# Rearranging the head of an RG-LRU and ConvFFN block: where modulation is applied, how the first product is cut, how the conditioning is spread

## The chip, the core and the metric

The kernel is one program on one core of a Trainium2 chip. The metric is the device time of one execution in microseconds (us), lower is better. Times are the median of several executions; the profile comes from one more execution of the same program.

## What is computed

One layer of a diffusion backbone: 256 context tokens and 1024 latent tokens of width 1024 go through an RMS norm, a shift and scale that depend on a conditioning vector, a bidirectional gated linear recurrence, and then a convolutional feed-forward part. Everything that the change touches stands in the first lines of it:

```python
silu_c, silu_cc = silu(c), silu(c_ctx)
sh1, sc1, g1, sh2, sc2, g2 = split(silu_c @ mod_w + mod_b, 6)      # 1024 values each
csh1, csc1, ...            = split(silu_cc @ mod_w + mod_b, 6)
h_lat = rms_norm(x)   * (1 + sc1)  + sh1
h_ctx = rms_norm(ctx) * (1 + csc1) + csh1
y_branch, x_branch = split(h @ w_in, 2)                            # 1280 columns each
xc = dwconv1d(x_branch)                                            # then gates, recurrence, gelu(y), w_out, FFN
```

## The kernel before

All products are made three times with operands split in a high and a low part (`hh`/`hl` for the activations, `wh`/`wl` for weights): high by high, low by high, high by low, summed in PSUM. Activations stand transposed: 128 of the 1024 channels on the partitions ("channel tile" k = 0 to 7), the 1280 tokens along the row (256 context, then 1024 latent).

The head (lines 183 to 315) runs under an order written out by hand for TensorE (PE), VectorE (DVE) and ScalarE (ACT); loads are issued in the program's order by SyncE (SP). It has these stages:

- **Conditioning rows** (L246 to L253, L277): DVE makes 16 diagonal tiles from `silu_c`, TensorE multiplies them with ones so that SiLU(c) and SiLU(c_ctx) stand on every partition, and four copies bring them from PSUM to the tiles `sh2` and `sc2`, which are free until later.
- **Norm and transposes** (L255 to L287): ten token tiles of 128 rows, in pairs. ACT squares and sums (L122), takes the root (L123), DVE refines it (L124, newton), DVE scales one tile of the pair (L267) and GpSimd (POOL) the other (L265), TensorE transposes (L270), and ACT and DVE copy the result from PSUM to `xT` (L231), a tile of 128 x 8 x 1280.
- **Modulation** of tile k (`mod_pe` L200, `mod_dve` L209): 16 pairs (k, shift or scale) are needed, each a product of a 1024 x 128 piece of `mod_w` with the two conditioning vectors. Seven pairs (`ON_PE`, L35) run on TensorE as eight matmuls 32 columns wide; nine run on DVE as two multiplications with a row sum (L213) and a small addition (L214).
- **Application and split** (`modulate`, L216): ACT applies shift and scale to context and latent part (L222, on `xT` in SBUF), rounds to `hh` (L223), and POOL, for tiles 6 and 7 DVE, makes `hl` (L85).
- **First product** `xp` (`k_step_late`, L162): per tile k nine matmuls over three chunks of tokens (512, 512, 256), first all with `hh,wh`, then `hh,wl`, then `hl,wh`. The first product of the other branch, `y0`, follows four tiles behind (`YLAG`, L313).

Then (L533) ACT takes `xp` into the convolution (L397), DVE adds the taps (L405), ACT and DVE split the result, the gates' products start (L423), `y0` goes through gelu (L388), the gates' sigmoids run (L434), and a long loop follows in which TensorE hardly pauses.

Of the kernel before, what the change touches and what calls it, by code (L numbers as in the profile page):

```python
# [11 lines left out]
F32 = mybir.dt.float32  # L12
# [7 lines left out]
P = 128  # L20
# [14 lines left out]
ON_PE = {(0, 0), (1, 0)} | {(k, 1) for k in (0, 1, 2, 4, 6)}  # L35
REP = 16

AHEAD_PE = 2
AHEAD_DVE = 2
YLAG = 4  # L40
LO_DVE = {6, 7}
# [25 lines left out]
def tile_kernel(ctx: ExitStack, tc: tile.TileContext, x, cx, par, mod_b, mod1, mod2, wyx, gw, w_out, w_up, w_down, fw, out):  # L67
# [39 lines left out]
    def newton(rs, sd, nv, between=lambda: None):  # L107

        V.reciprocal(rs, sd)
        between()  # L110
# [7 lines left out]
    def rstd_of(n, srcs, junks, between=lambda: None):  # L118
# [4 lines left out]
        ordered(act(sd, ss, AF.Sqrt, bias=eps, scale=1.0 / D))  # L123
        V.tensor_scalar(nv, ss, -0.5 / D, -0.5 * EPS, op0=ALU.mult, op1=ALU.add)  # L124
        newton(rs, sd, nv, between)
        return [rs[:, i:i + 1] for i in range(m)]

# [14 lines left out]
    ps_b = pool("ps_b", bufs=5, space=PSUM)  # L142
# [41 lines left out]
    xT = p0.tile([P, KD, NTOK], F32, name="xT")  # L184

    def head_load(src):
        t = p0.tile([P, D], F32, tag="ld", name="ld", bufs=8)
        load(t, src)
        return t

    def x_load(i):
        return head_load(cx[i * P:(i + 1) * P] if i < 2 else x[(i - 2) * P:(i - 1) * P])

    def mod_load(k):
        return [head_load(mod1[k, :, s * D:(s + 1) * D]) for s in range(2)]
# [4 lines left out]
    def mod_pe(k):  # L200
        for s in range(2):
            if (k, s) in ON_PE:
                i = 2 * k + s
                pm = pm_all[:, 2 * REP * i:2 * REP * (i + 1)]
                for kk in range(KD):
                    mm(pm.rearrange("p (r v) -> p r v", v=2), mr[k][s][:, kk * P:(kk + 1) * P], silu_c[:, kk].unsqueeze(1).to_broadcast([P, REP, 2]), kk == 0, kk == KD - 1)
                pms[k, s] = pm

    def mod_dve(k):  # L209
        for s in range(2):  # L210
            if (k, s) not in ON_PE:
                for v, row in enumerate((sh2, sc2)):
                    V.scalar_tensor_tensor(hl[KD - 1][:, :D], mr[k][s], 1.0, row, op0=ALU.mult, op1=ALU.mult, accum_out=md1[:, k, s, v:v + 1])  # L213
                V.tensor_scalar(md1[:, k, s], md1[:, k, s], mod_b1(k, s), None, op0=ALU.add)  # L214

    def modulate(k):  # L216
        for s in range(2):
            if (k, s) in ON_PE:
                act(md1[:, k, s], pms.pop((k, s))[:, :2], AF.Identity, bias=mod_b1(k, s))
        hf = xT[:, k]  # L220
        for v, t in ((1, slice(0, CTX)), (0, slice(CTX, NTOK))):
            act(hf[:, t], hf[:, t], AF.Identity, bias=md1[:, k, 0, v:v + 1], scale=md1[:, k, 1, v:v + 1])  # L222
        last[0] = S.copy(hh[k], hf).ins.name  # L223
        lo_part(V if k in LO_DVE else G, hl[k], hf, hh[k])

    def evac(p):

        for j, pts in zip((2 * p, 2 * p + 1), tps.pop(p)):
            for q, pt in enumerate(pts):
                o, pv = xT[:, 4 * q:4 * q + 4, j * P:(j + 1) * P], pt.rearrange("p (a b) -> p a b", a=4)  # L230
                (V.tensor_copy if j % 2 or q else S.copy)(o, pv)  # L231
                yield

    mr, pms, tps = {}, {}, {}

    def mod_start(k):
        mod_dve(k)
        mod_pe(k)

    with tc.manual_schedule(engines={ENG.PE, ENG.DVE, ENG.Activation}):  # L240
        act(silu_c, pr[:, C_C:].rearrange("p (t k) -> p k t", t=2), AF.Silu)

        act(stat[:, 0, :1], eps, AF.Sqrt)
        xts = [x_load(j) for j in range(4)]

        bp, _ = x_outs()  # L246
        bcs = [bp[:, :512], bp[:, 512:1024], bp[:, 1024:], bank()]
        for i, pb in enumerate(bcs):
            v, q = divmod(i, 2)
            for k in range(4):  # L250
# [665 lines left out]
```

## Time and profile before

| | us |
|---|---|
| median of 3 executions | 1283.44 (1283.37 to 1284.53) |
| the profiled execution | 1282.26 |
| its span in the profile | 1280.5 |
| TensorE busy | 1227.7 (96%) |
| VectorE busy | 1045.2 (82%) |
| ScalarE busy | 550.6 (43%) |
| GpSimd busy | 426.6 (33%) |
| mean granted TensorE clock | 0.982 of full |

The page's strip of 40 slices shows TensorE at 7, 8 or 9 tenths in the first three slices (32 us each) and nearly always 9 behind them. The head is the first 100 us; a row of the trace such as `79.43 1.42 ACT L397 ...` reads: start and length in us, engine, line, operation, output from inputs, shapes, and in brackets the idle time of the engine ahead of it and what ended that.

### The profile page before, as it was taken

How to read it: one execution, taken by the hardware profiler on the slowest of the kernel's cores; microseconds unless marked ns; L12 is line 12 of the kernel's file. 1: busy time of each engine (PE TensorE's matmuls, PEld its weight loads, DVE VectorE, ACT ScalarE, POOL GpSimd, SP SyncE). 2: the span in 40 equal slices, each digit the busy share in tenths (PEclk: the TensorE clock that was granted, in tenths of full speed). 3: DMA queues.
4: the chain of work that ended last, by engine and by line, in shares of the span. 5: the costliest groups of instructions: out<-in, count | busy, mean ns of one | idle time of the engine just before them, and what ended most of it. 6: DMA issues, size and time to landing. Idle time of an engine off the chain costs nothing.

```text
span 1280.5 us, 14366 instructions
## 1 busy us (share of the span) xinstructions
PE 1227.7 (96%) x5512; PEld 1000.2 (78%) x5512; DVE 1045.2 (82%) x1193; ACT 550.6 (43%) x707; POOL 426.6 (33%) x238
## 2 busy tenths in 40 slices
PE   7879999999998799999999999999999999999995
PEld 6758888888886578788888888888888888888873
DVE  7968999999988858679877777777777777777888
ACT  6568888888876234332222212222222222211344
POOL 4732222222223000252433333333333333334564
PEclk8799999999999899999999999999999999999999
DMA  8422333333334552221111111111111111111003
GB/s 319 176 82 83 123 124 124 123 124 123 108 99 149 193 171 79 66 83 50 35 48 50 50 50 50 50 50 50 50 50 47 39 38 43 50 50 50 17 1 131
DMA packets 56740, 108.74 MB, mean 85 GB/s; under 512 B 4568, under 2 KB 24024, under 8 KB 56672
## 3 DMA queue, kind: packets, MB, share of 16 engines
q1 hardware_dynamic: 56528, 107.57, 25.4%
q8 instruction: 43, 0.70, 0.2%
q10 hardware_dynamic: 144, 0.26, 0.1%
q14 instruction: 25, 0.20, 0.1%
HBM read 98.37 MB, written 9.44 MB: 84 GB/s over the span
## 4 chain that ended last, share of the span: by engine, by line
PE 83%; DVE 11%; ACT 3%; issue 2%; DMA 1%; POOL 0%; SPq 0%; DVEq 0%; ACTq 0%
PE u L88 38%; PE pd L88 20%; PE pb L88 14%; PE xp L88 10%; DVE hl L213 2%; DVE xc L405 1%; DVE md L214 1%; DVE stat L112 1%; DMA ld<-x_dram 1%; DVE rgl L85 1%; PE pt L720 0%; DVE x L790 0%; DVE b L461 0%; PE pb L270 0%; DVE o L860 0%
## 5 line engine op out<-in xcount | busy, mean ns | idle before, releaser
L757 DVE SCALAR_TENSOR_TENSOR acc<-u,pr,acc 128x945 f32<-128x945 f32 (+2 forms) x352 | 427.0, 1219 | 23.3 <-ACT acc L750 15.9
L88 PE MATMUL u<-h2h,wl 128*128 128x512 f32 x704 | 277.9, 395 | 0.0
L88 PE MATMUL u<-h2l,wh 128*128 128x512 f32 x704 | 277.4, 394 | 0.0
L88 PE MATMUL u<-h2h,wh 128*128 128x512 f32 x704 | 274.3, 390 | 0.2 <-ACT h2h L723 0.2
L85 POOL TENSOR_TENSOR wl<-raw,wh 128x1024 fp32r<-128x1024 f32 x66 | 161.6, 2449 | 329.1 <-ACT wh L150 311.1
L790 DVE TENSOR_TENSOR x<-pd,x 128x512 f32<-128x512 f32 x160 | 109.6, 685 | 128.6 <-PE pd L88 128.6
L88 PEld LDWEIGHTS u<-h2l,wh 128*128 128x128 f32 x704 | 132.4, 188 | 31.7 <-DVE h2l L85 0.4
L88 PEld LDWEIGHTS u<-h2h,wh 128*128 128x128 f32 x704 | 132.7, 189 | 31.1 <-ACT h2h L723 0.5
L88 PEld LDWEIGHTS u<-h2h,wl 128*128 128x128 f32 x704 | 132.4, 188 | 28.0
L88 PE MATMUL pd<-dh,gl 128*128 128x512 f32 x320 | 126.3, 395 | 0.0
L88 PE MATMUL pd<-dl,gh 128*128 128x512 f32 x320 | 126.2, 394 | 0.0
L88 PE MATMUL pd<-dh,gh 128*128 128x512 f32 x320 | 125.2, 392 | 0.0
L836 ACT CAST gh<-acc 128x1024 fp32r<-128x1024 f32 x22 | 23.1, 1050 | 223.7 <-DVE acc L833 223.7
L85 POOL TENSOR_TENSOR gl<-acc,gh 128x1024 fp32r<-128x1024 f32 x18 | 43.2, 2400 | 198.9 <-ACT gh L836 198.9
L832 ACT ACTIVATE acc<-acc 128x1024 f32<-128x1024 f32 x22 | 23.3, 1060 | 182.7 <-DVE acc L757 182.7
L150 ACT CAST wh<-raw 128x1024 fp32r<-128x1024 f32 x64 | 67.2, 1049 | 78.6 <-PE u L88 73.5
L88 PE MATMUL xp<-hh,wh 128*128 128x512 f32 (+1 forms) x240 | 84.9, 366 | 1.8 <-ACT hh L223 1.8
L88 PE MATMUL xp<-hl,wh 128*128 128x512 f32 (+1 forms) x240 | 82.0, 366 | 4.4 <-POOL hl L85 3.7
L88 PEld LDWEIGHTS pd<-dh,gl 128*128 128x128 f32 x320 | 60.0, 187 | 13.9
L88 PEld LDWEIGHTS pd<-dh,gh 128*128 128x128 f32 x320 | 60.1, 188 | 13.7
L88 PEld LDWEIGHTS pd<-dl,gh 128*128 128x128 f32 x320 | 60.0, 187 | 13.6
L769 POOL TENSOR_TENSOR dr<-dr,g 128x512 f32<-128x512 f32 x40 | 52.0, 1318 | 53.8 <-DMA dr<-w_down_dram 53.8
(188 smaller groups left out, 2284.6 us busy)
## 6 DMA issues: line engine op xcount, KB each, us to landing
raw<-w_up_dram SPq DMA_DIRECT2D x44, 512.0 KB, 3.4
mraw<-mod_dram SPq DMA_DIRECT2D x64, 256.0 KB, 4.4
raw<-wyx_dram SPq DMA_DIRECT2D x20, 512.0 KB, 3.6
dr<-w_down_dram SPq DMA_DIRECT2D x40, 256.0 KB, 4.4
ld<-mod_dram SPq DMA_DIRECT2D x16, 512.0 KB, 6.0
rgr<-rgd SPq DMA_DIRECT2D x16, 512.0 KB, 5.3
rgd<-r SPq DMA_DIRECT2D x10, 512.0 KB, 3.0
wor<-w_out_dram SPq DMA_DIRECT2D x10, 512.0 KB, 3.9
```

The source lines that it names most:

```text
L85: eng.tensor_tensor(lo, src, hi.bitcast(F32), op=ALU.subtract)
L88: T.matmul(o, w, r, start=start, stop=stop)
L112: V.scalar_tensor_tensor(sd, rs, rs, nv, op0=ALU.mult, op1=ALU.mult)
L150: S.copy(wh, raw)
L213: V.scalar_tensor_tensor(hl[KD - 1][:, :D], mr[k][s], 1.0, row, op0=ALU.mult, op1=ALU.mult, accum_out=md1[:, k, s, v:v + 1])
L214: V.tensor_scalar(md1[:, k, s], md1[:, k, s], mod_b1(k, s), None, op0=ALU.add)
L405: V.scalar_tensor_tensor(xc[:, oa:ob], xp[:, oa + s:ob + s], pr[:, C_CW + t * 4 + tap:C_CW + t * 4 + tap + 1], xc[:, oa:ob], op0=ALU.mult, ...
L757: V.scalar_tensor_tensor(o, uv[:, r0 + dy:r1 + dy, c0 + dx:c1 + dx], w(dy, dx), o, op0=ALU.mult, op1=ALU.add)
L769: G.tensor_tensor(raw, raw, g2[:, cs], op=ALU.mult)
L790: V.tensor_tensor(xs, pd, xs, op=ALU.add)
L832: ordered(act(aa, aa, AF.Silu))
L836: S.copy(gh, aa)
```

## The change

- The conditioning vectors come as a new input `cc`; two DMAs spread a row of 1024 values over the 128 partitions each, and ACT takes SiLU of the two tiles in place. The diagonal tiles, the ones products and the four copies are gone.
- `ON_PE` now holds (0, 0) and every (k, 1): nine pairs on TensorE, seven on DVE. Loads of `mod_w` pieces have five buffers of their own (`MODS`), token tiles ten. Pieces for tiles 0 and 1 are loaded ahead of, or between, the first four token tiles; the others two tiles ahead, with the later token tiles between them.
- Both halves of a token tile pair are scaled on DVE. The low parts of the activations and of the first two weights are made on DVE. POOL has no work in the head behind the identity.
- Nothing is copied from PSUM to `xT`: `turn(c, k)` transposes one channel tile of one chunk of tokens to PSUM, and `modulate(c, k, pt)` applies shift and scale from there to a small buffer `hf`, then rounds.
- The first product runs by chunks: chunk 0 for k = 0 to 7, chunk 1 from k = 3 on (`SECOND`), chunk 2 behind them. `y0` runs whole behind `xp`, one half of the latent tokens after the other.

```diff
-ON_PE = {(0, 0), (1, 0)} | {(k, 1) for k in (0, 1, 2, 4, 6)}
+ON_PE = {(0, 0)} | {(k, 1) for k in range(KD)}
+MODS = 5
+SECOND = {3: (0, 1), 4: (2, 3), 5: (4, 5), 6: (6,), 7: (7,)}
...
+    def turn(c, k):
+        a, n = CHUNKS[c]
+        pt = ps_h.tile([P, 512], F32, tag="pt", name="pt", bufs=4)
+        for i in range(n // P):
+            T.transpose(pt[:, i * P:(i + 1) * P], xts[a // P + i][:, k * P:(k + 1) * P], ident)
+        return pt
+
+    def modulate(c, k, pt):
+        a, n = CHUNKS[c]
+        hf = p0.tile([P, 512], F32, tag="hf", name="hf", bufs=3)
+        for v, lo, hi in ((1, a, min(a + n, CTX)), (0, max(a, CTX), a + n)):
+            if lo < hi:
+                act(hf[:, lo - a:hi - a], pt[:, lo - a:hi - a], AF.Identity, bias=md1[:, k, 0, v:v + 1], scale=md1[:, k, 1, v:v + 1])
+        last[0] = S.copy(hh[k][:, a:a + n], hf[:, :n]).ins.name
+        return hf
+
+    def low(c, k, hf):
+        a, n = CHUNKS[c]
+        lo_part(V, hl[k][:, a:a + n], hf[:, :n], hh[k][:, a:a + n])
...
+        for v, row in enumerate((sh2, sc2)):
+            load(row, cc[v:v + 1].to_broadcast([P, D]))
+            act(row, row, AF.Silu)
...
+        mod_load(0)
+        x_load(0)
+        x_load(1)
+        mod_load(1)
+        x_load(2)
+        x_load(3)
+        w_x = load_weight(NCH)
+        mod_pe(0)
+        mod_dve(0)
+        x_sums(0)
+        mod_pe(1)
+        x_scale(0)
+        mod_dve(1)
+        x_sums(1)
+        x_scale(1)
+        w_x = split(w_x, V)
...
+        for k in range(KD):
+            if k + 2 < KD:
+                mod_load(k + 2)
+            if k in (0, 1):
+                x_load(2 * k + 4)
+                x_load(2 * k + 5)
+            if k == 5:
+                x_load(8)
+                x_load(9)
+            if k == 6:
+                w_y = load_weight(0)
+            pt = turn(0, k)
+            hf = modulate(0, k, pt)
+            if 0 < k < KD - 1:
+                mod_pe(k + 1)
+                mod_dve(k + 1)
+            flush()
+            low(0, k, hf)
+            for kk in SECOND.get(k, ()):
+                pt = turn(1, kk)
+                hf = modulate(1, kk, pt)
+                low(1, kk, hf)
+                later.append(lambda kk=kk: x_step(1, kk))
+            x_step(0, k)
+            if k in (1, 2, 6):
+                p = {1: 2, 2: 3, 6: 4}[k]
+                x_sums(p)
+                x_scale(p)
+        pts = {k: turn(2, k) for k in range(2)}
+        flush()
+        for k in range(KD):
+            hf = modulate(2, k, pts.pop(k))
+            low(2, k, hf)
+            if k + 2 < KD:
+                pts[k + 2] = turn(2, k + 2)
+            x_step(2, k)
+        w_y = split(w_y, V)
...
+        for q in range(2):
+            for k in range(KD):
+                k_step(y0[q:q + 1], YS[q:q + 1], w_y, k)
```

`x_sums` is the squares and the root of a pair of token tiles, `x_scale` the refinement and the two scalings; `flush` issues the products of chunk 1 that were put off. Behind the head the instructions of all engines are the same and stand in the same order.

Two places show what moves. On TensorE, around channel tile 4 (`hh_94` is its high part, `hl_102` its low part, `hh_90` and `hl_98` are tile 0; `xp` is the first product, `pb` the other branch), before:

```order
L88 MATMUL xp<-hh_94,wh 128x512 x2
L88 MATMUL xp<-hh_94,wh 128x256
L88 MATMUL xp<-hh_94,wl 128x512 x2
L88 MATMUL xp<-hh_94,wl 128x256
L88 MATMUL xp<-hl_102,wh 128x512 x2
L88 MATMUL xp<-hl_102,wh 128x256
L88 MATMUL pb<-hh_90,wh 128x512
L88 MATMUL pb<-hl_98,wh 128x512
```

and now (`pt` takes transposes of token tiles; `pm` takes the modulation's products):

```order
L231 MATMUL pt<-ident,xt 128x128 x8
L86 MATMUL xp<-hh_94,wh 128x512
L86 MATMUL xp<-hh_94,wl 128x512
L86 MATMUL xp<-hl_102,wh 128x512
L231 MATMUL pt<-ident,xt 128x128 x4
L86 MATMUL pm<-silu_c,mr 128x32 x8
L86 MATMUL xp<-hh_92,wh 128x512
L86 MATMUL xp<-hh_92,wl 128x512
L86 MATMUL xp<-hl_100,wh 128x512
```

Nine products of one channel tile in a row have become three for chunk 0, with the transposes of the next tile right behind the product that needs the low part, and no product of the other branch between them. On ACT, around channel tiles 3 and 4, before (`md_71` holds shift and scale):

```order
L222 ACTIVATE xT<-xT,md_71 128x256
L222 ACTIVATE xT<-xT,md_71 128x1024
L223 CAST hh_93<-xT 128x1280
L219 ACTIVATE md_71<-pb,pr 128x2
L222 ACTIVATE xT<-xT,md_71 128x256
L222 ACTIVATE xT<-xT,md_71 128x1024
L223 CAST hh_94<-xT 128x1280
```

and now, from the two chunk-1 tiles (2 and 3) that go along with tile 4 to tile 5 of chunk 0:

```order
L240 CAST hh_94<-hf 128x512
L209 ACTIVATE md_71<-pm,pr 128x2
L239 ACTIVATE hf<-pt,md_71 128x512
L240 CAST hh_92<-hf 128x512
L239 ACTIVATE hf<-pt,md_71 128x512
L240 CAST hh_93<-hf 128x512
L239 ACTIVATE hf<-pt,md_71 128x256 x2
L240 CAST hh_95<-hf 128x512
```

Three instructions for a whole channel tile have become seven for its three chunks, spread over the head, and each now waits for a transpose.

## Rows read from the trace of the kernel before

**Rows 1.** Chain of waits in the first 100 us, shares by engine and line.
```profile
by line: DVE hl L213 31.8%; DVE md L214 9.6%; DMA ld<-x_dram 7.5%; PE pb L88 7.1%; PE xp L88 6.2%; PE pb L270 5.4%; DVE xc L405 4.8%; DVE xT L231 2.5%; POOL ld L265 2.4%; issue 2.2%; DVE ld L267 1.5%; ACT xh L411 1.4%; ACT xc L397 1.4%; DVE
```

**Rows 2.** A stretch: length; busy us of PE, PEld, DVE, ACT, POOL; clock, DMA share, GB/s.
```profile
40.00:60.00 20.00, 14.59 (x67) 12.48 (x66) 19.75 (x18) 8.72 (x10) 15.51 (x5) 0.76 0.38 127
```

**Rows 3.** Timeline, DVE's modulation and POOL's low parts, 50 to 61 us.
```profile
50.06 1.22 DVE L213 SCALAR_TENSOR_TENSOR hl<-ld,sh 128x1024 fp32r<-128x1024 f32 x1
52.72 1.22 DVE L213 SCALAR_TENSOR_TENSOR hl<-ld,sh 128x1024 fp32r<-128x1024 f32 x1
53.29 7.29 POOL L85 TENSOR_TENSOR hl<-xT,hh 128x1280 fp32r<-128x1280 f32 x2 [4.49 <-ACT hh L223]
53.99 3.80 DVE L213 SCALAR_TENSOR_TENSOR hl<-ld,sc 128x1024 fp32r<-128x1024 f32 x1
57.83 2.77 DVE L214 TENSOR_SCALAR md<-md,pr 128x2 f32<-128x2 f32 x1
```

**Rows 4.** Timeline, ACT and PE from the end of the first product.
```profile
79.43 1.42 ACT L397 ACTIVATE xc<-xp,pr 128x1280 f32<-128x1280 f32 x1 [2.52 <-PE xp L88]
85.71 0.63 PE L88 MATMUL pb<-hh,wl 128*128 128x512 f32 x2
88.56 1.09 ACT L388 ACTIVATE gy<-pb 128x512 f32<-128x512 f32 x2
93.54 1.63 ACT L434 ACTIVATE r<-pb,pr 128x512 f32<-128x512 f32 x3
94.28 0.38 PE L88 MATMUL pb<-xh,gwh 128*128 128x256 f32 x1 [2.16 <-ACT r L434]
```

**Rows 5.** Loads: one piece of the chain, and two stretches as in Rows 2.
```profile
2.58 7.54 DMA ld<-x_dram
10.00:12.00 2.00, 1.06 (x8) 0.85 (x8) 1.31 (x2) 1.93 (x7) 2.00 (x1) 1.00 1.03 420
531.00:532.00 1.00, 1.00 (x4) 0.81 (x3) 0.85 (x2) 1.00 (x3) 0.00 (x0) 0.50 0.99 283
```

**Rows 6.** Timeline, from the second square of the first pair to the first scaling.
```profile
7.60 1.06 ACT L122 ACTIVATE hh<-ld 128x1024 fp32r<-128x1024 f32 x1 [0.98 <-DMA ld<-cx_dram]
9.89 0.75 DVE L267 TENSOR_SCALAR ld<-ld,stat 128x1024 f32<-128x1024 f32 x1
```

**Rows 7.** Groups by shape: count, busy us and mean ns of one, idle ahead.
```profile
L750 ACT ACTIVATE acc<-u,pr 128x1024 f32<-128x1024 f32 x44 | 52.8, 1200 | 2.7 <-PE u L88 2.7
L397 ACT ACTIVATE xc<-xp,pr 128x1280 f32<-128x1280 f32 x10 | 14.2, 1417 | 2.5 <-PE xp L88 2.5
L411 ACT CAST xh<-xc 128x512 fp32r<-128x512 f32 x20 | 11.4, 619 | 6.0 <-DVE xc L405 6.0
L85 DVE TENSOR_TENSOR xl<-xc,xh 128x512 fp32r<-128x512 f32 x20 | 12.9, 688 | 2.1 <-ACT xh L411 1.5
```

**Rows 8.** Timeline, PE: transposes, narrow products, products in threes at either clock.
```profile
23.48 1.09 PE L270 MATMUL pb<-ident,ld 128*128 128x128 f32 x8 [0.59 <-POOL ld L265]
24.41 3.66 PE L88 MATMUL pb<-silu_c,ld 128*128 128x32 f32 x32
45.25 0.75 PE L88 MATMUL xp<-hl,wh 128*128 128x512 f32 x3
45.84 0.75 PE L88 MATMUL xp<-hh,wh 128*128 128x512 f32 x3
59.14 1.27 PE L88 MATMUL xp<-hl,wh 128*128 128x512 f32 x3
60.21 1.27 PE L88 MATMUL xp<-hh,wh 128*128 128x512 f32 x3
```

**Rows 9.** Stretches as in Rows 2, for the clock.
```profile
28.00:30.00 2.00, 1.99 (x13) 1.62 (x13) 0.67 (x1) 1.42 (x2) 0.00 (x0) 0.63 0.93 350
44.00:46.00 2.00, 2.00 (x12) 1.73 (x12) 2.00 (x3) 0.00 (x0) 2.00 (x2) 1.00 0.46 162
58.00:60.00 2.00, 2.00 (x8) 1.61 (x7) 2.00 (x1) 0.00 (x0) 2.00 (x1) 0.50 0.00 0
```

More of the change, by code (lines that the diff above doesn't have):

```diff
@@ L66, in tile_kernel @@
 @with_exitstack
[L67 removed]
+def tile_kernel(ctx: ExitStack, tc: tile.TileContext, x, cx, cc, par, mod_b, mod1, mod2, wyx, gw, w_out, w_up, w_down, fw, out):
     nc = tc.nc
@@ L123, in rstd_of, with rms_dve @@
         ordered(act(sd, ss, AF.Sqrt, bias=eps, scale=1.0 / D))
+    def rms_dve(n, m):
+        ss, nv, sd, rs = (stat[:, i, n:n + m] for i in range(4))
         V.tensor_scalar(nv, ss, -0.5 / D, -0.5 * EPS, op0=ALU.mult, op1=ALU.add)
-        newton(rs, sd, nv, between)
+        newton(rs, sd, nv)
         return [rs[:, i:i + 1] for i in range(m)]
+    def rstd_of(n, srcs, junks):
+        rms_act(n, srcs, junks)
+        return rms_dve(n, len(srcs))
     dr = ctx.enter_context(tc.tile_pool(name="dr", bufs=1, space=bass.MemoryType.DRAM))
@@ L183, in tile_kernel, with x_load @@
     p0 = pool("p0")
[L184 to L192, printed above, removed]
+    def x_load(j):
+        t = p0.tile([P, D], F32, tag="xt", name="xt", bufs=10)
+        load(t, cx[j * P:(j + 1) * P] if j < 2 else x[(j - 2) * P:(j - 1) * P])
+        xts[j] = t
     def mod_load(k):
-        return [head_load(mod1[k, :, s * D:(s + 1) * D]) for s in range(2)]
+        for s in range(2):
+            mr[k, s] = t = p0.tile([P, D], F32, tag="mr", name="mr", bufs=MODS)
+            load(t, mod1[k, :, s * D:(s + 1) * D])
     def mod_b1(k, s):
@@ L212, in mod_dve @@
                 for v, row in enumerate((sh2, sc2)):
-                    V.scalar_tensor_tensor(hl[KD - 1][:, :D], mr[k][s], 1.0, row, op0=ALU.mult, op1=ALU.mult, accum_out=md1[:, k, s, v:v + 1])
+                    V.scalar_tensor_tensor(hl[KD - 1][:, :D], mr[k, s], 1.0, row, op0=ALU.mult, op1=ALU.mult, accum_out=md1[:, k, s, v:v + 1])
                 V.tensor_scalar(md1[:, k, s], md1[:, k, s], mod_b1(k, s), None, op0=ALU.add)
[L216 to L238, printed above, removed]
+    def x_sums(p):
+        js = (2 * p, 2 * p + 1)
+        rms_act(2 * p, [xts[j] for j in js], [junk] * 2)
@@ L243, in tile_kernel @@
         act(stat[:, 0, :1], eps, AF.Sqrt)
[L244 to L250, printed above, removed]
-                dg = xT[:, i, k * P:(k + 1) * P]
-                V.tensor_scalar(dg, ident, silu_c[:, 4 * q + k, v:v + 1], None, op0=ALU.mult)
-                mm(pb[:, k * P:(k + 1) * P], ones, dg, True, True)
-        pm_all = bank()
@@ L303, in tile_kernel @@
[L303 to L314 removed]
+        pm_all = ps_h.tile([P, 512], F32, tag="pm", name="pm")
+        xp, xo0 = x_outs()
@@ new lines, in tile_kernel, with flush @@
+        junk = p0.tile([P, D], F32, tag="junk", name="junk")
+        mod_load(0)
[14 more added lines that the diff above has]
+        w_x = split(w_x, V)
+        later = []
+        def flush():
+            for f in later:
+                f()
+            later.clear()
```

81 lines of the change are left out of this document (14 added, 67 removed).

## The prediction

> **What bounds the kernel now.** I read the strip of 40 slices first: TensorE is short of work only in the first 100 us. So the question is when the dense part begins, and one event marks it: the first gate product that waits for a sigmoid, at 94.28 [rows 4]. From there on both kernels issue the same instructions in the same order and TensorE hardly pauses, so a shift of that event is the change of the time. Then the chain of waits [rows 1]: of the first 100 us 31.8% are DVE's L213 and 9.6% L214, the modulation's multiplications. A quiet pair (k, shift or scale) costs DVE 52.72 - 50.06 = 2.66 us; beside POOL's subtractions one multiplication takes 3.80 instead of 1.22 and the small addition 2.77, until POOL's instruction ends [rows 3]. Nine pairs should take 24 us, the chain gives them 41. DVE is therefore the bound in the middle of the head: 19.75 busy of 20 us, where ACT has 8.72 and TensorE runs at 0.76 of its clock [rows 2].
>
> **What goes, what comes, step by step.**
>
> *The start.* Before, the parameters and four tiles of 512 KB had landed at 2.58 + 7.54 = 10.1 us [rows 5]. Now the first five loads are the parameters, the two spread rows and the two pieces of tile 0: the same bytes to SBUF, so again 10.1 if a spread row goes like a tile. The only nearby stretch with a repeated source moved 283 GB/s where plain tiles reach 420 [rows 5]: 1.85 us a row instead of 1.25, 1.2 us for both; I take the lower price, since that stretch was shared with smaller loads, and keep +1.2 for the range. Six more loads at 1.25 us bring the pieces of tile 1 at 15.1 and the fourth token tile at 17.6. TensorE's eight narrow products of tile 1 (0.114 each [rows 8], at half clock 0.2) and the small ACT copy end at 17.1; ACT, in order, then takes two squares, and root, refinement and two scalings follow: a square of about 1.2, 2.3 from the start of the second to the scaling [rows 6], 1.5 for the scalings. First transposes at about 22.5, where before they came at 11. This wait for loads, with the modulations set between the token tiles, is the price of knowing the modulation early. The diagonal tiles, ones products and four copies that go, and the two SiLU that come (some 1.1 each on ACT), lie under these loads and count nothing; without that cover the SiLU would cost 2.2.
>
> *DVE.* Seven pairs are left, 7 x 2.66 = 18.6; low parts, 0.69 per 512 columns [rows 7], come to 11 for chunks 0 and 1 and 3 for chunk 2; five pairs of tiles are refined and scaled for some 2.3 each; two weights about 1.2 each. Together 47 where nothing of POOL holds it up, against 41 for the modulation alone before. The 17 us lost to POOL are gone, 12 of them are spent again on POOL's former work.
>
> *ACT.* Here the new bound forms. Activations out of PSUM with shift and scale: 1.200 for 1024 columns and 1.417 for 1280 [rows 7] give 0.77 for 512 and 0.55 for 256. With the cast (0.62 for 512, by the same slope 0.40 for 256) and an overlap of 0.1 between neighbours: chunk 0 (two of 256) 1.55, chunk 1 1.30, chunk 2 0.88 per channel tile; times eight 29.8. Six squares and three roots are still inside the loop, 8.4, and six small copies of the modulation, 1.0. Total 39.2 behind the first transposes.
>
> *The hand-offs.* ACT cannot work without a pause, since TensorE takes its instructions in order: transposes of tile k+1 stand behind the third product of tile k, which waits for DVE's low part. From ACT's cast to its next activation: 0.69 + a product + four transposes (1.09 for eight [rows 8]) + three hand-offs, 1.7 at full clock and 2.4 at half, where a group of three products takes 1.07 instead of 0.59 [rows 8]. Behind k = 0 this stands open, about 2.5. Behind k = 1 two squares cover it. At k = 2 DVE has the scaling of a pair and a modulation (5 us) ahead of the low part, the squares cover half: 2.6 open. For k = 3 to 6 the two chunk-1 tiles cover most of it, 1.2 open each, 5 in all. The entry to chunk 2 costs 1.1, its eight steps 0.1 each. Sum 12.
>
> So `xp` ends at 22.5 + 0.9 (first transposes) + 39.2 + 12 + 0.9 (last low part and product) = 75.5, against 79.4, where ACT takes it over [rows 4]: 3.9 us won.
>
> *The other branch gives most of it back.* Before, four of the eight tiles of `y0` lay in the pauses of the first product, and it ended at 85.71 + 0.63 = 86.3, 6.9 behind `xp`. Now all 48 products stand behind `xp`: 48 x 0.235 (0.59 buys 512, 512 and 256 columns) = 11.3; the weight's cast is the last of ACT's queue and its low part behind that on DVE, 1.3 until both are there. End 75.5 + 12.6 = 88.1, 1.8 later than before. Convolution, taps and split (8 us) lie under it. That DVE's subtraction for this weight stands ahead of the taps delays nothing TensorE waits for.
>
> *The end.* Before, from the end of the gelu (89.65) to the first sigmoid (93.54) 3.9 us of casts and table loads passed, and the gate product came 0.74 behind [rows 4]. Now the first half of `y0` is done 5.6 earlier, so table load and first gelu are over and only the second, 0.6, follows the end: 88.1 + 0.65 + 3.9 + 0.74 = 93.4. Against 94.28 that is 0.9 us won.
>
> *What costs nothing.* Pieces of `mod_w` wait for buffers that are freed one or two steps earlier, and the last two token tiles stand behind them in SP's queue, but are wanted two steps (10 us) later; cover gone, a load is 3 us. The loads of the long loop that stand ahead of the next weight in SP's queue delay it by some 3 us; TensorE wants it 14 us after `xp`.
>
> The profiled execution took 1282.26 (its span 1280.5), the median of three is 1283.44; a shift of 0.9 makes the two 1281.4 and 1282.5.
>
> **TensorE's clock is the large unknown.** In the trace it stands at half (0.50) at 58 to 60 us and at full at 44 to 46, and it fell at 28 to 30, behind 3.7 us of narrow products [rows 8, 9]. At full clock a step of k = 3 to 5 asks TensorE for 12 transposes, 8 narrow and 9 wide products: 1.4 + 0.9 + 2.1 = 4.4 us, beneath ACT's 5.4 with its pause; at half about 8, and TensorE is the bound: +2.5 a step. Before, unbroken groups of nine products stood at either clock (full at 45, half at 59 [rows 8, 9]); the first three steps now have three each, with pauses, so I take half clock until about 45 us and full behind it. If it is full from the start, the open hand-offs shrink and step 3 is shorter: 4.5 us better. If it comes back only at 60, three steps lose 2.5 less what pauses they had, about 5.5; at 70 or later chunk 2 and the first half of `y0` also suffer, 9.
> The Trainium skill (TensorE: Matmul & The Clock Gate, "HAM oscillation — how this bites in real kernels") says that bursts of products separated by waits fall back to the slow clock again and again, and advises long runs without waits; this change cuts runs up. Taken strictly, it gives the slow rival below; the trace so far bears it out in part, since products with pauses ran at full clock from 44 to 46.
>
> **Rivals.** (1) *Faster: the clock holds early.* It is back by 25 to 33 us, hand-offs run at the shorter price: 2.6 to 5.4 us won, 1278.0 to 1280.8. For it: from step 3 on transposes and products leave few pauses. Against it: the first three steps are thin, and squares and scalings lie between. Chance 0.33.
> (2) *Slower: the clock stays at half through steps 3 to 5.* TensorE becomes the bound of the loop; it decides from a return later than about 53 us: 2.6 to 8 us lost, 1286.0 to 1291.5. For it: narrow products stand in each step; a fall stands behind such ones [rows 9]. Against it: a TensorE that is the bound is also busy without pause, and before the full clock of 44 to 46 it had been so [rows 9]. Chance 0.19.
> (3) *The modulation is not known ahead.* Loads decide: if spread rows take 1.85 or more and pieces come later than the tiles, the first transposes move to 24 or 25 and DVE's chain is still what ACT waits for: 2 us more than forecast, 1284.5, a little slower than before but within the bound. Chance 0.06.
> (4) *Forecast:* -0.9, with hand-offs and durations 2 us off either way, 1280.9 to 1286.0. Chance 0.42.
>
> **How the numbers follow.** About 0.2%, 2.6 us, is what a measurement of this kernel can tell from no change. Faster: rival 1 and a bit of the forecast's edge, 0.34. Slower: rival 2 and the edge of 3, 0.21. Same: 0.45. The range runs from rival 1's end, 1278.0, into rival 2 up to 1287.5, which leaves out about a tenth there and less below. I predict 1282.5.
>
> **What would show it.** First transposes near 22.5 (later than 24: rival 3). ACT's idle time between 23 and 76 near 12, most of it ended by transposes. `xp` over at 75.5, `y0` 12.6 behind it. No multiplication of DVE over 1.3 in the head. The granted clock near 0.5 up to 45 and 1.0 behind. The forecast is wrong if the first waiting gate product starts outside 91.7 to 96.9, or if anything behind it differs between the two traces by more than 1 us.

## The result: slower by 0.56%, and the profile after

The changed kernel took 1290.99 us (median of 4, 1288.64 to 1291.55) against 1283.4 (4, 1282.21 to 1284.53): ratio 1.0056, 95% interval 1.0038 to 1.0073. The forecast was 1282.5 with a range of 1278.0 to 1287.5. The profiled execution took 1291.4, its span is 1289.6 (before 1282.26 and 1280.5), 9.1 us more. One execution of a later run, with one scale pair more on TensorE, took 1370.11 at a granted clock of 0.84 and is left out of that run's numbers.

The event that the forecast watched, the first gate product that waits for a sigmoid, came at 103.12 in place of 94.28 [rows 4]: 8.84 later, so nearly the whole difference lies ahead of it. The event is not the time itself, though: behind it the profiled executions of the kernels below take 1183.9 to 1187.7 us (before 1186.2, after 1186.5), so a shift of the event can differ from the shift of the time by up to some 2 us, and both are given. The timeline of ACT and TensorE from the end of the first product, after (start, duration, instruction, idle time and what ended it):

```profile
85.52 1.42 ACT L411 ACTIVATE xc<-xp,pr 128x1280 f32<-128x1280 f32 x1
...
97.88 0.60 ACT L402 ACTIVATE gy<-pb 128x512 f32<-128x512 f32 x1 [2.62 <-PE pb L86]
...
103.12 0.39 PE L86 MATMUL pb<-xh,gwh 128*128 128x256 f32 x1 [0.36 <-ACT r L448]
```

The first product is handed over at 85.52, ten us later than the 75.5 of the forecast; from there on the distances are those of the forecast. So the miss lies in the start and in the loop over the channel tiles. The chain of waits of the first 100 us, after, says where to look; it stands against [rows 1]:

```profile
by line: PE pm L86 21.2%; PE pb L86 11.0%; DMA mr<-mod_dram 8.7%; PE xp L86 8.0%; ACT hf L239 8.0%; PE pt L231 6.6%; issue 5.1%; DVE hl L215 4.8%; DMA xt<-x_dram 4.8%; ACT junk L119 4.6%; DVE xt L224 3.6%; DVE hl L83 2.5%; ACT wh L154 2.0%;
```

DVE's multiplications fell from 31.8% to 4.8% (L215), as intended. In their place stands `pm`, 21.2%: the narrow products on TensorE that compute the modulation, which the forecast had as a small cost. The stretches of the loop (length; busy us and count of PE, PEld, DVE, ACT, POOL; clock, DMA share, GB/s) answer to [rows 2]:

```profile
20.00:40.00 20.00, 13.63 (x54) 11.51 (x53) 12.73 (x32) 11.69 (x24) 0.00 (x0) 1.00 0.66 257
40.00:60.00 20.00, 18.16 (x94) 16.36 (x94) 15.30 (x31) 12.30 (x24) 0.00 (x0) 1.00 0.49 154
60.00:80.00 20.00, 16.48 (x91) 12.58 (x91) 13.45 (x27) 16.00 (x32) 0.00 (x0) 0.91 0.20 78
```

From 40 to 60 us DVE went from 19.75 to 15.30 and TensorE from 14.59 to 18.16: most of the work moved from DVE to TensorE. ACT, which the forecast took for the new bound, has 12.30 of 20 there.

Now TensorE's timeline, after: the three narrow groups of the start, the first transposes, three of the loop's narrow groups, and two neighbouring wide products at either clock:

```profile
10.91 3.59 PE L86 MATMUL pm<-silu_c,mr 128*128 128x32 f32 x16 [10.91 <-DMA mr<-mod_dram]
14.86 3.62 PE L86 MATMUL pm<-silu_c,mr 128*128 128x32 f32 x16 [0.35 <-ACT md L209]
18.83 3.62 PE L86 MATMUL pm<-silu_c,mr 128*128 128x32 f32 x16 [0.35 <-ACT md L209]
...
23.04 1.05 PE L231 MATMUL pt<-ident,xt 128*128 128x128 f32 x2 [0.59 <-DVE xt L224]
...
28.46 0.47 PE L231 MATMUL pt<-ident,xt 128*128 128x128 f32 x1 [0.19 <-DVE xt L224]
...
32.99 3.46 PE L86 MATMUL pm<-silu_c,mr 128*128 128x32 f32 x16
...
51.73 0.63 PE L86 MATMUL xp<-hh,wl 128*128 128x512 f32 x1
52.16 0.63 PE L86 MATMUL xp<-hl,wh 128*128 128x512 f32 x1
...
56.14 0.40 PE L86 MATMUL xp<-hl,wh 128*128 128x512 f32 x1
56.38 0.39 PE L86 MATMUL xp<-hh,wh 128*128 128x512 f32 x1
...
59.09 1.87 PE L86 MATMUL pm<-silu_c,mr 128*128 128x32 f32 x16
...
65.29 1.87 PE L86 MATMUL pm<-silu_c,mr 128*128 128x32 f32 x16
```

Read the counts at the line ends. One pair (one tile, shift or scale) is eight calls in the source, and x16 in the trace. So the "eight matmuls" of a pair in the description of the kernel before are sixteen for TensorE. A pair costs 1.87 at full clock and 3.46 to 3.62 at half, where the forecast had 0.9 and 1.6 (eight at 0.114 and at 0.2). The row to see it in was there before: the group by shape of the narrow products, of before and of after, has 112 for seven pairs and 144 for nine.

```profile
L88 PE MATMUL pb<-silu_c,ld 128*128 128x32 f32 x112 | 16.9, 315 | 4.2 <-ACT md L219 4.2
```

```profile
L86 PE MATMUL pm<-silu_c,mr 128*128 128x32 f32 x144 | 27.3, 359 | 11.6 <-DMA mr<-mod_dram 10.9 <-ACT md L209 0.7
```

### The profile page after: what moved, and what is told of

The parts are those of the page before. It is cut to its first block, busy times and chain, and to the rows that moved or that the text cites. A ratio compares the mean times of both kernels' runs of the same rounds, so it can differ in the third digit from the quotient of the medians.

```text
span 1289.6 us, 14368 instructions
## 1 busy us (share of the span) xinstructions
PE 1234.5 (96%) x5512; PEld 1003.9 (78%) x5512; DVE 1027.1 (80%) x1179; ACT 557.1 (43%) x736; POOL 387.1 (30%) x225
## 4 chain that ended last, share of the span: by engine, by line
PE 86%; DVE 7%; ACT 3%; DMA 2%; issue 2%; SPq 0%; POOL 0%; DVEq 0%; ACTq 0%
PE u L86 38%; PE pd L86 20%; PE pb L86 15%; PE xp L86 10%; PE pm L86 2%; DMA mr<-mod_dram 1%; DVE stat L109 1%; ACT hf L239 1%; PE pt L734 1%; DVE x L804 1%; DVE rgl L83 1%; PE pt L231 1%; DVE b L475 0%; DVE o L874 0%; DVE xc L419 0%
## 5 line engine op out<-in xcount | busy, mean ns | idle before, releaser
L83 POOL TENSOR_TENSOR wl<-raw,wh 128x1024 fp32r<-128x1024 f32 x64 | 156.8, 2449 | 323.9 <-ACT wh L154 300.1
L86 PE MATMUL xp<-hh,wh 128*128 128x512 f32 (+1 forms) x240 | 89.1, 371 | 4.3 <-ACT hh L240 4.2
L86 PE MATMUL xp<-hl,wh 128*128 128x512 f32 (+1 forms) x240 | 85.2, 368 | 2.9 <-DVE hl L83 2.9
L783 POOL TENSOR_TENSOR dr<-dr,g 128x512 f32<-128x512 f32 x40 | 52.2, 1324 | 58.5 <-DMA dr<-w_down_dram 50.1
```

The source lines that it names most:

```text
L83: eng.tensor_tensor(lo, src, hi.bitcast(F32), op=ALU.subtract)
L86: T.matmul(o, w, r, start=start, stop=stop)
L783: G.tensor_tensor(raw, raw, g2[:, cs], op=ALU.mult)
```

## The experiments

Theory N: the narrow groups are the miss. They cost twice the forecast; three of them stand in a row in the start, one more stands ahead of the wide products in each of the steps k = 1 to 6, and the longer half-clock stretch is their consequence. The rivals: C, the first product cut in threes, with a hand-off behind each three, is what costs; L, the loads of the spread rows; K, half of the loss is the slow clock of the thin first steps. Each experiment is an edit of the changed kernel unless it says otherwise.

**Half of the narrow products.** Every second product of a pair is left out, and with it half of the modulation's sum; the run is for its time alone.

```diff
-                for kk in range(KD):
+                for kk in range(0, KD, 2):
...
-... kk == 0, kk == KD - 1)
+... kk == 0, kk == KD - 2)
```

> The changed kernel with every second of the eight partial products of a modulation pair on TensorE left out (the modulation is therefore not the reference's), so that a pair is 8 recorded narrow products instead of 16, which is what the forecast counted. Theory N (the forecast's miss is this count: the trace of before has 112 narrow products for seven pairs, 16 each): a pair takes about 1.75 us at half clock instead of 3.6, the first transposes of the last token tile move from 28.5 to about 23 to 24.5, xp ends near 76.5 instead of 85.5, the first gate product that waits for a sigmoid starts near 94.5 instead of 103.1, and the time is 1281 to 1285. Rival C (the first product cut in threes with a hand-off behind each is what costs): that product starts at 100 or later, the time is 1287 or more. Rival L (the loads of the spread rows): the start moves by less than 2 us.

Measured: 1282.73 (8 runs), ratio 0.9997 (0.9986 to 1.0007). Its narrow products by shape, and from the timelines the first pair, the transposes of the fourth token tile, the first narrow group at full clock, the hand-over of the first product, the second gelu and the event:

```profile
L86 PE MATMUL pm<-silu_c,mr 128*128 128x32 f32 x72 | 13.9, 350 | 12.2 <-DMA mr<-mod_dram 11.9 <-ACT md L209 0.4
```

```profile
9.65 1.88 PE L86 MATMUL pm<-silu_c,mr 128*128 128x32 f32 x8 [9.65 <-DMA mr<-mod_dram]
...
23.78 0.47 PE L231 MATMUL pt<-ident,xt 128*128 128x128 f32 x1 [0.18 <-DVE xt L224]
...
45.27 0.98 PE L86 MATMUL pm<-silu_c,mr 128*128 128x32 f32 x8
...
75.44 1.42 ACT L411 ACTIVATE xc<-xp,pr 128x1280 f32<-128x1280 f32 x1
...
87.81 0.60 ACT L402 ACTIVATE gy<-pb 128x512 f32<-128x512 f32 x1 [2.63 <-PE pb L86]
...
93.05 0.39 PE L86 MATMUL pb<-xh,gwh 128*128 128x256 f32 x1 [0.36 <-ACT r L448]
```

With the count that the forecast used, the forecast's steps come out: 75.44 for 75.5, 87.8 for 88.1, 93.05 for 93.4, 1282.7 for 1282.5. That they agree so closely is in part luck: the fourth token tile's transposes come at 23.78 for 22.5, and the loop behind them is as much shorter than forecast. ACT's wait for transposes, which was to be near 12 between 23 and 76, is 12.5 from 22 to 76. The clock is back at about 45, as forecast, and not at 55: its late return in the changed kernel followed from the groups. C is out, which wanted the event at 100 or later, and L, which wanted the start moved by less than 2 us: the fourth tile's transposes moved by 4.7. Theory N holds for nearly all of the miss: against the kernel before, measured beside each, the medians are 7.6 us above (changed kernel), 0.1 above (this run) and 0.9 below (forecast), so 7.5 of 8.5 us. The event moves by 10.1, of which 1.3 are loads that came earlier in this profiled execution (9.65 for 10.91).

**Two columns in place of 32.** The run above takes away products and work alike. This one keeps the count:

```diff
-REP = 16
+REP = 1
```

> The changed kernel with 2 columns in place of 32 in each narrow product; nothing is left out, the number of products stays (16 recorded to a pair). Theory W (a narrow product is paid by its columns): a pair falls to under half, 0.9 at full and under 1.8 at half clock, and the loss goes as in the run with half the products: event 92 to 95, time 1281 to 1284. Theory F (a price for each instruction, whatever its columns): a pair stays at 1.5 to 1.9 at full and 3 to 3.6 at half, event 101 to 104, time 1289 to 1291.5. Rival C (with so few columns the clock stays at half longer): a pair shorter, but products 0.43 apart beyond 55 us, event over 98.

Measured: 1290.17 (4 runs), ratio 1.0059 (1.0042 to 1.0076), event 102.29. The group by shape, one pair at full clock with its weight loads (PEld is TensorE's weight load), and the weight loads of such a pair in the changed kernel with its 32 columns:

```profile
L86 PE MATMUL pm<-silu_c,mr 128*128 128x2 f32 x144 | 26.7, 316 | 10.4 <-DMA mr<-mod_dram 9.7 <-ACT md L209 0.7
```

```profile
57.48 1.84 PE L86 MATMUL pm<-silu_c,mr 128*128 128x2 f32 x16
57.37 1.86 PEld L86 LDWEIGHTS pm<-silu_c,mr 128*128 128x128 f32 x16
```

```profile
58.98 1.87 PEld L86 LDWEIGHTS pm<-silu_c,mr 128*128 128x128 f32 x16
```

A sixteenth of the columns, and a pair costs 1.84 in place of 1.87: theory F. What a narrow product costs is not its columns. Its stationary operand is a piece of `mod_w` of 128 x 128 that no other product uses, and sixteen loads of weights fill the same 1.86 us without a gap. That fits a price per load of weights of 0.116 at full clock (1.86 / 16) and some 0.22 at half (3.46 and 3.62 / 16). It is an inference: a fixed price for each such product, whatever its weights, fits as well, since no run here took the loads away and kept the products. The Trainium skill (TensorE: Matmul & The Clock Gate, "LDWEIGHTS (loading the stationary operand)") says that a load is paid by the columns of the weights; by its formula 128 of them are an estimate of 128 / 1.2 = 107 ns. If the price is the load's, the 0.116 at full clock agrees roughly, the 0.22 at half does not.

**The start in another order.** Token tiles are loaded ahead of the pieces, and the sums of both pairs of tiles stand ahead of the narrow groups:

```diff
-        mod_load(0)
         x_load(0)
         x_load(1)
-        mod_load(1)
+        mod_load(0)
         x_load(2)
         x_load(3)
+        mod_load(1)
         w_x = load_weight(NCH)
-        mod_pe(0)
-        mod_dve(0)
         x_sums(0)
-        mod_pe(1)
         x_scale(0)
-        mod_dve(1)
         x_sums(1)
         x_scale(1)
+        mod_pe(0)
+        mod_dve(0)
+        mod_pe(1)
+        mod_dve(1)
```

> The changed kernel with the order of its start alone changed: token tiles 0 and 1, then the pieces of channel tile 0, tiles 2 and 3, pieces of tile 1; squares and scalings ahead of the modulation on ACT and DVE. Theory N: the squares no longer stand on ACT behind the copies of three narrow pairs, first transposes at 23 to 24 instead of 28.5, the loop behind is unchanged, the first waiting gate product 4 to 5 us earlier (98 to 99.5), time 1286 to 1287.5. Rival C (hand-offs of the loop set the end): the loop gives the start back, the product moves by less than 1.5 us, time 1289.5 to 1291.

Measured: 1288.71 (5 runs), ratio 1.0041 (1.0026 to 1.0055).

```profile
24.46 1.09 PE L231 MATMUL pt<-ident,xt 128*128 128x128 f32 x4
...
61.20 1.93 PE L86 MATMUL pm<-silu_c,mr 128*128 128x32 f32 x16
...
63.95 0.63 PE L86 MATMUL xp<-hl,wh 128*128 128x512 f32 x1
64.38 0.63 PE L86 MATMUL xp<-hh,wh 128*128 128x512 f32 x1
...
100.85 0.38 PE L86 MATMUL pb<-xh,gwh 128*128 128x256 f32 x1 [0.40 <-ACT r L448]
```

The transposes of the fourth token tile come 4.0 earlier (24.46 for 28.46), the event 2.3: between what the two theories expected. The 4.0 last to the end of the loop: its last narrow group starts at 61.20 for 65.29. Behind it products stand 0.43 apart (63.95, 64.38), at half clock, where the changed kernel had its full clock, and 1.7 us are lost (from the fourth tile's transposes to the event 100.85 - 24.46 = 76.4 against 103.12 - 28.46 = 74.7). So what the start won lasted, and the clock took part of it back in this execution, the slowest of the five; the others were not profiled. How much the order wins is less sure: in three later runs that keep the changed kernel's start the same transposes came at 26.54, 26.96 and 27.11, so it is 2.1 to 4.0. What it is due to stays open between the loads, ACT's squares behind copies that wait for narrow groups, and DVE's scalings behind a modulation, since the edit moves all three.

**The clock alone.** Fourteen wide products on constants ahead of the loop, into `xp` before it is used:

```diff
         w_x = split(w_x, V)
+        for _ in range(14):
+            mm(xp[:, :512].rearrange("p (r v) -> p r v", v=P), ones_r, ones_r.unsqueeze(1).to_broadcast([P, 4, P]), True, True)
```

> The changed kernel with 14 wide products (ones by ones, into a bank that the first product overwrites) on TensorE between the narrow pairs of tiles 0 and 1 and the first transposes, where TensorE waits for the scalings: at half clock 14 x 0.43 = 6 us, from 22.5 to 28.5, so nothing waits for them. If the slow clock of the first five steps is half of the loss (theory K): products in the loop start at full clock (0.235 apart instead of 0.43) at once, a narrow pair takes 1.87 instead of 3.46 in steps 1 to 4, and the first waiting gate product comes 4 to 8 us earlier, at 95 to 99, time 1283 to 1287. If the narrow pairs pull the clock down again at once (N with its own clock effect), the full clock lasts one or two steps at most and the product comes 0 to 3 us earlier.

Measured: 1288.27 (3 runs), ratio 1.0045 (1.0029 to 1.0061).

```profile
20.77 4.83 PE L86 MATMUL xp<-ones_r 128*128 128x512 f32 x14
...
30.12 0.65 PE L231 MATMUL pt<-ident,xt 128*128 128x128 f32 x4
30.56 3.47 PE L86 MATMUL pm<-silu_c,mr 128*128 128x32 f32 x16
...
100.84 0.39 PE L86 MATMUL pb<-xh,gwh 128*128 128x256 f32 x1 [0.39 <-ACT r L450]
```

The fillers did bring the full clock: four transposes in 0.65 in place of 1.05. Right behind them it was gone, the narrow group takes 3.47. Of the 2.28 us by which the event is earlier, 1.5 are loads (the first pair could begin at 9.41 instead of 10.91 in this execution); the full clock, while it lasted, gave some 0.8. So warming ahead of this loop does not last, as in the second case; that the narrow groups pull the clock down is not shown, since pauses came before the first of them. What a clock held at full through the first steps would be worth, and with it theory K, this run can't tell; by the run with half of the products the loss goes with the count, at a clock that is still at half up to 45.

**The spread rows alone, in the kernel before.** The diagonals, ones products and copies go, the two rows are loaded spread ahead of the token tiles (`xts = [x_load ...` stands behind them):

```diff
+        for v, row in enumerate((sh2, sc2)):
+            load(row, cc[v:v + 1].to_broadcast([P, D]))
+            act(row, row, AF.Silu)
...
-        bp, _ = x_outs()
-        bcs = [bp[:, :512], bp[:, 512:1024], bp[:, 1024:], bank()]
-        for i, pb in enumerate(bcs):
-            v, q = divmod(i, 2)
-            for k in range(4):
-                dg = xT[:, i, k * P:(k + 1) * P]
-                V.tensor_scalar(dg, ident, silu_c[:, 4 * q + k, v:v + 1], None, op0=ALU.mult)
-                mm(pb[:, k * P:(k + 1) * P], ones, dg, True, True)
...
-            if p == 1:
-                for i, pb in enumerate(bcs):
-                    (S.copy if i < 2 else V.tensor_copy)((sh2, sc2)[i // 2][:, i % 2 * 512:i % 2 * 512 + 512], pb)
```

> The kernel before with one part of the change alone: the two spread conditioning rows come by DMA ahead of the token tiles and pass a SiLU, and the sixteen diagonals, their products with ones and the four copies out of PSUM are gone. Theory Z (the part is nearly free, as the forecast had it: the work that it removes lay beside the loads of the tokens, and what it adds is 1 MB of load): the token tiles land 3 to 4 us later, part of which the idle time behind the start takes up; event (first gate product that waits for a sigmoid) between 94.0 and 96.5 against 94.28, time 1282.5 to 1285. Theory D (the loads set the start, and all of it is passed on): event 97.5 to 98.5, time 1286 to 1287. Theory G (the removed diagonals and copies stood in DVE's and TensorE's way): event before 93.5, time under 1282.

Measured: 1287.36 (4 runs), ratio 1.0034 (1.0021 to 1.0046). First transposes of before, then first transposes and event of this run, and ACT's SiLU of the second row and its first square:

```profile
10.79 1.06 PE L270 MATMUL pb<-ident,ld 128*128 128x128 f32 x8 [0.85 <-DVE ld L267]
```

```profile
15.05 4.43 PE L266 MATMUL pb<-ident,ld 128*128 128x128 f32 x24 [15.05 <-DVE ld L263]
...
97.51 0.39 PE L88 MATMUL pb<-xh,gwh 128*128 128x256 f32 x1 [2.10 <-ACT r L427]
```

```profile
8.21 1.06 ACT L245 ACTIVATE sc<-sc 128x1024 f32<-128x1024 f32 x1 [0.87 <-DMA sc<-cc_dram]
...
10.81 1.06 ACT L122 ACTIVATE hh<-ld 128x1024 fp32r<-128x1024 f32 x1
```

The start moves by 4.3, the event by 3.2, the median by 4.2 (1283.2 for the kernel before beside it): nearest to theory D, at the lower edge of its event and a little over its time. This part of the change is a loss by itself, whatever the diagonals that it replaces were worth. But the loads are not the whole of it: the squares do not wait for token tiles. They stand on ACT behind the SiLU of the second row, which starts when that row has landed, at 8.21, and a table load; the second square is at 11.87, where it was at 7.60 [rows 6]. How much of the price is load and how much SiLU, the run does not divide. In the changed kernel the two SiLU cost nothing, as forecast: ACT is idle for 2.58 us behind them, until the first narrow group is done.

**Two scale pairs back on DVE.** If TensorE is full, DVE has room by the stretches above (12.73 and 15.30 of 20):

```diff
-ON_PE = {(0, 0)} | {(k, 1) for k in range(KD)}
+ON_PE = {(0, 0)} | {(k, 1) for k in (0, 1, 3, 5, 6, 7)}
```

> The changed kernel with the scale pairs of tiles 2 and 4 back on DVE: TensorE loses two of its groups of sixteen narrow products of the half-clock stretch (3.46 each), DVE gains two pairs of 2.66. DVE was busy 12.7 of 20 us from 20 to 40 and 15.3 from 40 to 60. Theory N (TensorE's narrow groups, each twice as long as forecast, carry the loss of the loop): two of them gone give 2 to 4 us, event 99 to 101 against 103.12, time 1287 to 1289. Rival (DVE has no room there and takes the place of TensorE): event 102.5 to 105, time 1290.5 to 1293.

The same with the other order of the start:

> The changed kernel with both: the start in the order of the earlier experiment (token tiles first, sums of both pairs ahead of the conditioning) and the scale pairs of tiles 2 and 4 on DVE. If the two losses are separate and add, the event comes at 97 to 99 against 103.12 and the time is 1285 to 1287; what then is left to the 1282.6 of the kernel before is the first token pieces behind the spread rows and the clock that stays at half longer. If they share one cause (DVE or ACT is next late in the loop), event 100 to 101 as with the start alone, time 1288 to 1289.

Measured: 1294.81 (4 runs), ratio 1.0093 (1.0078 to 1.0107), event 105.66; with the start reordered 1292.68 (4 runs), ratio 1.0076 (1.0063 to 1.0089), event 105.31. Both expectations of a gain were wrong; the first went the rival's way and past its bounds, though its loads were 1.9 us earlier than in the changed kernel (9.00 for 10.91), and the second is worse than either case named. The busy stretches hid it. DVE's and TensorE's timelines of the first run, at step k = 3:

```profile
45.34 1.22 DVE L215 SCALAR_TENSOR_TENSOR hl<-mr,sh 128x1024 fp32r<-128x1024 f32 x1
...
49.26 1.22 DVE L215 SCALAR_TENSOR_TENSOR hl<-mr,sc 128x1024 fp32r<-128x1024 f32 x1
...
50.66 1.89 DVE L83 TENSOR_TENSOR hl<-hf,hh 128x512 fp32r<-128x512 f32 x3
```

```profile
51.41 0.79 PE L86 MATMUL xp<-hl,wh 128*128 128x512 f32 x1 [3.75 <-DVE hl L83]
...
60.96 0.45 PE L86 MATMUL xp<-hh,wl 128*128 128x512 f32 x1
```

With two pairs in one step DVE's low part waits 5.3 us behind them, and TensorE 3.75 us for the low part; and TensorE, with more pauses, has its full clock back only at about 61. DVE's idle time lay in the wrong steps. These two steps had no room for the extra pair on DVE; other tiles were not tried.

**The low parts of the kernel before on DVE.** What [rows 3] said of the kernel before can be had alone: the low parts go from POOL to DVE, nothing else.

```diff
-LO_DVE = {6, 7}
+LO_DVE = set(range(8))
...
-        w_x = split(w_x, G)
+        w_x = split(w_x, V)
...
-                w_y = split(w_y, G)
+                w_y = split(w_y, V)
```

> The kernel before with one part of the change alone: low parts of the activations and of the first two weights on DVE instead of POOL, so that behind the transposes POOL does nothing in the head. Theory P (17 us of DVE's chain were lost to POOL's subtractions): no multiplication over 1.3 us behind 32 us; DVE then has nine pairs at 2.66 and eight low parts of 1.49 and two of 1.2, 38 us, from 32: xp ends at 73 to 75 instead of 79.4, time 1278 to 1280. Rival: low parts behind the modulation of two tiles ahead make the products wait, DVE stays the chain, xp ends at 78 or later, time 1282 to 1286.

Measured: 1278.51 (4 runs), ratio 0.9962 (0.9947 to 0.9977), faster than both kernels. A low part on DVE and one of its multiplications, the stretch, and the event:

```profile
49.45 1.49 DVE L85 TENSOR_TENSOR hl<-xT,hh 128x1280 fp32r<-128x1280 f32 x1
...
53.52 1.22 DVE L213 SCALAR_TENSOR_TENSOR hl<-ld,sh 128x1024 fp32r<-128x1024 f32 x1
```

```profile
40.00:60.00 20.00, 15.28 (x81) 12.41 (x80) 19.61 (x32) 11.88 (x14) 0.00 (x0) 0.93 0.42 145
```

```profile
88.97 0.39 PE L88 MATMUL pb<-xh,gwh 128*128 128x256 f32 x1 [2.16 <-ACT r L434]
```

DVE takes over 1.49 us of work from POOL per tile, no multiplication is over 1.23 from 35 to 68 us, and the event is 5.3 earlier; the median is 4.1 below the 1282.59 of the kernel before beside it. DVE still fills its stretch (19.61 of 20), which suggested the next step: scale pairs moved from DVE to TensorE on top of this, those of tiles 3 and 5, and of tile 3 alone.

```diff
-ON_PE = {(0, 0), (1, 0)} | {(k, 1) for k in (0, 1, 2, 4, 6)}
+ON_PE = {(0, 0), (1, 0)} | {(k, 1) for k in (0, 1, 2, 3, 4, 5, 6)}
```

> The kernel before with all low parts on DVE (as in the run before) and in addition the scale pairs of tiles 3 and 5 on TensorE: DVE loses two pairs of 2.66 us from its unbroken stretch of 40 to 68 us, TensorE gains two groups of sixteen narrow products (1.87 each at full clock, 3.6 at half). Theory Q (DVE is still the chain of that stretch, and TensorE has room, 32.6 busy of 40 us): the first product ends 2 to 4 us earlier than 74.1, event 85.5 to 87.5 against 88.97, time 1275 to 1277. Rival (TensorE has become the chain; narrow groups stand ahead of the products as in the changed kernel): event 88.5 to 91, time 1278 to 1281.

> The same kernel as the run with the scale pairs of tiles 3 and 5 on TensorE, to see a usual execution in place of the fastest of twelve. If the head differs, its event lies at 89 to 92 in place of 84.55 with narrow groups at 3.6 in place of 1.87 behind 44 us. If the head is the same (event within 0.5 of 84.55), the 7 us are lost behind it, at a lower granted clock (0.978 to 0.981 over the whole span, against 0.987).

> The kernel before with all low parts on DVE, and one scale pair more on TensorE (that of tile 3 alone; the run with tiles 3 and 5 profiled at 1273.6 but lay at 1280.4 in the median). If what the second pair cost in most executions is TensorE's share of the head, one pair gives a median of 1276 to 1278, against 1278.5 with none. If any added group of narrow products puts the clock at half for longer in most executions, 1279 to 1281.

Measured, with two pairs more: 1280.36 (12 runs, 1273.62 to 1282.22), ratio 0.9976 (0.9965 to 0.9986). The profiled execution of that run and a second one of the same kernel are the quickest, 1273.6 and 1274.8, with narrow groups at 1.87 from 44 and 45 us on, and the event at 84.55 and 85.72. In the first TensorE is busy 20.00 of 20 us:

```profile
40.00:60.00 20.00, 20.00 (x116) 17.69 (x116) 16.79 (x27) 15.64 (x20) 0.00 (x0) 0.91 0.44 150
```

```profile
84.55 0.58 PE L88 MATMUL pb<-xh,gwh 128*128 128x256 f32 x1 [2.18 <-ACT r L434]
```

The eleven timed executions took 1277.2 to 1282.2, at a mean granted clock of 0.977 to 0.985 against 0.987 in the profiled ones. So the mechanism of theory Q shows in the two profiles, the median doesn't have it, and where the timed executions lost it stays open, since both profiles show a quick one. With one pair: 1278.5 to 1281.6 in nine executions, ratio 0.9979 (0.9969 to 0.9988). That is the time of the second case, but its reason, a longer half clock, is not shown: none of the nine has a profile. The three intervals overlap, so no gain of the added pairs is shown, and the version to take is the simplest, which only moves the low parts.

## Why the prediction was wrong

**The step that failed** is one count. The forecast wrote "TensorE's eight narrow products of tile 1 (0.114 each [rows 8], at half clock 0.2)". The 0.114 is right (3.66 / 32), the eight is the count of calls in the source; the trace records sixteen to a pair. The row that the price came from, `x32` in 3.66 [rows 8], is two pairs; at eight to a pair it would be four. Every place that counts narrow products inherits it:

- *The start.* The three groups that stand in a row took 3.6 each, 11.5 from 10.91 to 22.45, where the forecast had tile 1 done at 17.1. ACT's squares stand behind the copies that wait for them. First transposes of the fourth tile at 28.46, with the smaller count at 23.78, forecast 22.5 for all four tiles. Of the 4.7 between the two runs 1.3 are loads that came later in the one profiled (10.91 against 9.65).
- *The loop.* The forecast's step of k = 3 to 5, 12 transposes, 8 narrow and 9 wide products in 4.4 us at full clock, should have been 5.4, as much as ACT's 5.4, and at half some 10 in place of 8. The steps k = 1 to 3 were hit hardest: 3.46 of narrow group ahead of the wide products. From the transposes of the fourth tile to the event it is 74.7 us against 69.3 with half the count (93.05 - 23.78): 5.4 us. In ACT's waits from 23 to 76 us, 11.9 are for transposes (forecast 12) and 4.8 more for narrow groups, which the forecast had at none.
- *The clock.* Forecast "half clock until about 45 us and full behind it"; products are 0.43 apart up to 52.2 and 0.24 apart from 56.1, and at half once more from 74.7 to 78 (0.91 in the stretch from 60 to 80), as with half of the products from 65.6 to 68.6. Rival 2 named a return later than about 53 us and gave it 1286.0 to 1291.5: the outcome, 1290.99, lies in it, TensorE became the bound of the loop (one wait over 1 us, of 1.84, between 31 and 64), and narrow products in each step were among its reasons. But its price was of the forecast's count. A return at about 54 would have put the time near 1286 by it; the other 5 us are the start, which it did not move, and the doubled groups. That the time lies in its range is luck.

These places add up to the miss: event 103.12 against 93.4, and 93.05 with the count as forecast (8.8 of the 10.1 us when the loads' 1.3 are taken off).

**What was right.** DVE's chain is gone: seven pairs at 1.22 or 1.23 a multiplication, none drawn out by POOL. The steps of ACT (two of 256 in 1.02 where 1.0 was implied by 0.55 each less the overlap, 0.60 for the gelu). `y0` behind `xp`: the second gelu stands 97.88 - 85.52 = 12.4 behind the hand-over, 12.6 forecast; from it to the event 5.24, 5.29 forecast. Behind the event the two traces differ by 0.3 us (1289.6 - 103.12 = 1186.5 and 1280.5 - 94.28 = 1186.2).

**What was slightly off.** The first loads, "again 10.1", let the first narrow group start at 10.91 in the profiled execution, at 9.00 and 9.65 in others with the same order of loads; the +1.2 that was kept for the range covers it. The forecast read in the trace that "products with pauses ran at full clock from 44 to 46"; in [rows 9] TensorE is busy for 2.00 of those 2.00 us, so that row says nothing about pauses, as rival 2 had it. Rival 3 (loads decide) had its sign: late transposes, but by products, not by loads.

**What remained hidden in the sum.** Had a pair cost what the forecast counted, the change was still no gain: the run with half the narrow products only draws level (0.9986 to 1.0007). By the two runs on the kernel before, spreading the rows by DMA costs 4.2 us of the median (3.2 of the event), and keeping the low parts off POOL wins 4.1 (5.3 of the event). The change contains both, and alone they cancel. How much `y0` behind `xp` and the two more pairs on TensorE take of it was not measured by itself.

## What to carry to other kernels

Take the number of instructions of a step from the count that the trace gives for it (112 for seven pairs), not from the calls in the source, and check it by dividing a group's count by the number of pairs. A recorded f32 product with a fresh 128 x 128 stationary operand costs 0.116 us at full clock here, with 32 columns and with 2; many small ones are no filler but a block of 1.87 to 3.62 us in TensorE's order. And when a profile says that one engine slows another (3.80 for 1.22), try that edit alone before a rewrite that contains it: it was worth 0.38%.

## What the runs showed of the hardware that was not expected

- The recorded clock can be wrong at the start of a trace. After, the stretches read 1.00 from 20 to 60 us, while wide products at 51.73 and 52.16 stood 0.43 apart, twice the 0.24 of 56.14 and 56.38. The distance between like products is the better sign. The Trainium skill (TensorE: Matmul & The Clock Gate, "Seeing it yourself") warns that recorded clock events on this chip have been seen to be unreliable; these rows agree.
- A full clock can be lost within one step: at 30.12 four transposes in 0.65, and the narrow group at 30.56, right behind, in 3.47 as at half clock, after 4.83 us of dense products and 5 us with pauses. Nor is it the same in each run: with the other order of the start and with two columns products stand 0.43 apart again around 64 and 67 us, in the changed kernel at 0.24.
- Loads with a repeated source seem slower than plain ones. In the stretch from 4 to 6 us, where the two spread rows are among the loads under way, the eight profiled executions that have them moved 244 to 320 GB/s, the four with plain tiles alone 328 to 406. From 6 to 8 us the two groups overlap (272 to 418 and 334 to 416), and no stretch holds spread rows alone. The slowest of each, after and before:

```profile
4.00:6.00 2.00, 0.00 (x0) 0.00 (x0) 0.00 (x0) 0.31 (x1) 0.00 (x0) 1.00 0.92 244
```

```profile
4.00:6.00 2.00, 1.62 (x7) 1.63 (x8) 1.97 (x10) 1.96 (x3) 0.00 (x0) 1.00 0.96 328
```

- The end of the first loads varies between executions by almost 2 us: the first narrow group, which waits for them, began at 10.91, 9.65, 9.41, 9.67 and 9.00 in five runs that load in the same order.
